# Merging two score stretches of an attention head, with other chains held back around them

## The chip, the core and the metric

The kernel runs on one core of a Trainium2 chip. The core's engines run side by side, each in its own order: PE (TensorE, matrix products; its weight loads are listed as PEld), DVE (VectorE), ACT (ScalarE), POOL (GpSimd), and SP, which issues DMAs. PE writes its products into PSUM, which has eight banks; DVE and ACT read them from there. The metric is the time of one execution in microseconds of device time, the median of several runs. A profiled execution gives, for every instruction, its start and length.

## The reference

One decoder layer, on 512 tokens of width 1024, in float32:

```
x = x + 0.5 * swiglu(rms_norm(x), ...)                  # first FFN
x = x + hybrid_mixer(rms_norm(x), ...)                  # state space part beside attention
x = x + memory_cross_attention(rms_norm(x), ...)
x = x + 0.5 * swiglu(rms_norm(x), ...)                  # second FFN
return rms_norm(x, norm_final_w)
```

The change concerns the mixer. Its attention has 8 heads; each head has two sets of queries and keys (c = 0, 1) of width 64 and a value of width 128:

```
logits = einsum('bqhcd,bkhcd->bhcqk', q_blk, k) * scale + bias   # causal, by blocks of 128 queries
p = softmax(logits)
w = p[:, :, 0] - lam * p[:, :, 1]
out = einsum('bhqk,bkhe->bqhe', w, v)
```

The other half of the mixer is a state space scan with 16 heads in 4 groups, by chunks of 128 tokens, with a gated norm over each group at its end.

## The kernel before

All products in float32 are made from operands split into a high and a low part (names that end in h and l), three products in place of one: high by high, high by low, low by high. ACT makes the high part and DVE the low one. Weights come in tiles of 128 x 1024 (wr), are split into wh and wl, and feed 24 products of 512 columns each; three wh and wl buffers stand in a row.

PSUM is cut into four banks "acc" for the large projections and four banks "aux" for everything small: scores, transposes, states, norms.

**The order of the work** comes from the class Order. It holds a list of dense generators (the projections, which yield about every second product) and a list of chains (the small work that depends on them). A chain yields how long it wants to rest; each entry of the list is a due time and the generator. The clock od.t advances with each product by a modelled cost, (columns + 8) / 2400 us for split operands, four times that for plain float32 products, and 2 x (128 + 8) / 2400 us for a transpose. The loop in run() first takes ready[0], the first chain of the list that is due, in order of spawning, and otherwise the next dense step. What is written first has the higher priority when the instructions are laid out; PE, DVE and ACT can still be given another order where an operand isn't there in time by the planner's reckoning. SP and POOL keep the written order.

**A head** is a chain (head, line 766), spawned 3.4 us after its queries and keys are projected. Its steps, with the rest between them: scores of block 3 (512 keys); 3.3; scores of block 2 (384 keys) and combine(3); 3.3; scores of blocks 1 and 0 (256 and 128 keys), combine(2) and turn(3); 3.3; combine(1), combine(0) and turn(2); 3.3; turn(1); 2.0; turn(0); 3.3; the product with the values (po); 2.08; a transpose (ptk) for the norm; 6.75; a transpose back (pot). scores (line 770) takes two aux banks, one for each c, and makes for each block three products for each c. The operands of c = 0 lie in partitions 0 to 63, those of c = 1 in 64 to 127: these are products over 64 rows, and two of them run side by side. Behind them DVE adds the bias and takes the extreme of each row (line 787), and ACT makes the exponentials and their sums (line 788). combine joins the two softmaxes on DVE, turn transposes the weights into an aux bank (pt) and splits them out of it.

A projection of queries and keys takes PE some 11 us, so the end of one head's chain lies beside the beginning of the next.

**A group** of the scan is a chain too (group, line 928). For each of its two halves j it makes decay factors on ACT and DVE (names gate and th, line 993), rests 6.9 us (2.0 more for j = 0, 0.5 more for j = 1 of group 2), and makes the products pf and py. Later sums_by_token (nps) gives the squares of each token, inv_rms_cols takes a power on POOL (ncol, line 368), and row_of (line 371) rests and then spreads the result by four transposes (nrow). DVE scales y by it (line 1028), and the parts of ys are split. The last output projection (out_proj) reads ys: of its first two tiles the first six k steps run ahead, and the last two wait for group 3.

Other chains in the same list: conv (three steps on DVE for each tile of the scan's inputs, which read an acc bank), steps (the time steps of the scan), and block_sums_in_dram, which makes sums of weight tiles in DRAM for the second FFN with a DMA on SP and an adding DMA on POOL for each.

Of the kernel before, what the change touches and what calls it, by code (L numbers as in the profile page):

```python
# [14 lines left out]
ALU = mybir.AluOpType  # L15
AX = mybir.AxisListType

P = 128
T = 512
# [18 lines left out]
W = {"h0": 3.4, "hs": 3.3, "ht": 2.0, "hv": 2.08, "hp": 6.75}  # L38
# [18 lines left out]
class Order:  # L57
# [5 lines left out]

    def __init__(self):
        self.t = 0.0
        self.dense = []
        self.chains = []

# [12 lines left out]
    def run(self):  # L81
        blocked = None
        while self.dense or self.chains:
            ready = [c for c in self.chains if c[0] <= self.t]
            if ready:
                self.step(ready[0])
                continue
            if blocked is not None and blocked():
                blocked = None
            if self.dense and blocked is None:  # L90
                try:
                    blocked = next(self.dense[0])
                except StopIteration:
                    self.dense.pop(0)
                continue
            c = min(self.chains, key=lambda c: c[0])
            self.t = max(self.t, c[0])
            self.step(c)


def body(tc, a, dbg=None):
# [31 lines left out]
    def aux(s, shape=(P, T)):  # L133
        return aux_p.tile(list(shape), F32, tag="aux", name=nm(s))
# [6 lines left out]
    V, S, G = nc.vector, nc.scalar, nc.gpsimd  # L141
    od = Order()

    def mm(out, w, x, start, stop, share=1.0):
        od.t += share * (1 if w.dtype == R32 else 4) * (x.free_size() + 8) / 2400
        newest_mm[:] = [nc.tensor.matmul(out, w, x, start=start, stop=stop).ins]  # L146
# [189 lines left out]
    for k in range(KT):  # L336
# [3 lines left out]
        w = s2("wa")  # L340
# [425 lines left out]
    def head(hd, q, kq, bias):  # L766
        es, w0, w1 = {}, {}, {}
        sm = [small("sm", 4) for _ in range(2)]

        def scores(*blocks):  # L770
            ps = [aux("ps") for _ in range(2)]
            parts, to = {}, 0
            for i in blocks:
                n = P * (i + 1)
                parts[i] = slice(to, to + n)
                to += n
                for j, (u, w) in enumerate(((0, 0), (0, 1), (1, 0))):
                    for c in range(2):
                        pc = slice(64 * c, 64 * c + 64)
                        mm(ps[c][:, parts[i]], q[u][pc, i * P : (i + 1) * P], kq[w][pc, :n], j == 0, j == 2)  # L780
            for i in blocks:
                n = P * (i + 1)
                es[i] = []
                for c in range(2):
                    ec = s2("ec", shape=(P, n))
                    mn = small("mn", 1, bufs=8)
                    V.tensor_tensor_reduce(out=ec[:, :n], in0=ps[c][:, parts[i]], in1=bias[:, T - n :], scale=0.125, scalar=3e38, op0=ALU.add, op1=ALU.min, accum_out=mn)  # L787
# [23 lines left out]
                w0[j], w1[j] = s2("wt", R32, (P, n)), s2("wt", R32, (P, n))  # L811
            split_into(w0[j], w1[j], pt[:, :n])

        scores(3)
        yield W["hs"]
        scores(2)
        combine(3)
        yield W["hs"]
        scores(1, 0)
        combine(2)  # L820
        turn(3)
        yield W["hs"]
# [12 lines left out]
        hs = slice((hd % 4) * P, (hd % 4 + 1) * P)  # L835
# [92 lines left out]
    def group(g, bt, ct, xs, zs):  # L928
# [52 lines left out]
        for j in range(2):  # L981
# [3 lines left out]
            for hh in range(2):  # L985
# [5 lines left out]
                    S.activation(r[:, c], r[:, c], AF.Relu, bias=cum[:, c, hd : hd + 1], scale=-1.0)  # L991
                S.activation(r, r, AF.Exp, scale=-1.0)
                V.tensor_tensor(r, r, cbm, ALU.mult)
            yield W["gd"] + (W["gt"] if j == 0 else 0.5 if g == 2 else 0.0)
            pf = aux("pf")
            with behind(list(newest_mm)):
                for c in range(1, 4):
# [24 lines left out]
        yield W["gq"] + (1.2 if g == 2 else 0.0)  # L1022
        pn = yield from sums_by_token(sq[0], 4)
        rh = inv_rms_cols(pn, 4, 4.0 / (4 * 256), 4.0 * EPS)
        pr = yield from row_of(rh, 4, W["gn"] + 1.1)
        for j in range(2):
            n = 2 * g + j
            V.scalar_tensor_tensor(yz[j], yz[j], par[:, C_SSD + n : C_SSD + n + 1], pr, ALU.mult, ALU.mult)
# [643 lines left out]
```

## Time and profile before

| | |
|---|---|
| median of 3 runs | 1290.15 us (1289.37 to 1290.36) |
| the profiled execution | 1289.51 us |
| its span, first to last instruction | 1287.7 us |
| granted PE clock, mean | 0.997 |
| 378 to 490 us (heads 0 to 3): PE, DVE, ACT busy | 111.97, 76.88, 62.17 us of 112 |
| 560 to 650 us (heads 4 to 7): PE, DVE, ACT busy | 90.00, 67.87, 53.56 us of 90 |
| 760 to 800 us (end of the groups): PE, DVE, ACT busy | 39.41, 31.90, 25.08 us of 40 |

A line of the timeline gives the start in us from the span's start, the length in us, the engine, the line of the kernel, the operation, what it writes and reads, the shapes (for PE the rows x columns of the array that it uses, and the moving operand), and how many like instructions the line joins. Idle time ahead of it stands in brackets with what ended it. A line of groups ends with the busy time, the mean length in ns, and the idle time ahead. Products overlap: the next one starts before the last has ended, so the length of a joined line is more than the distance to the next line.

### The profile page before, as it was taken

Reading aid. Unit: us, or ns where it says so; the run is one execution under the profiler, and the core shown is the slowest. Engines: PE = TensorE matmul, PEld = TensorE weight load, DVE = VectorE, ACT = ScalarE, POOL = GpSimd, SP = SyncE. Lnnn points to the kernel's source line nnn. Section 1 sums busy time; section 2 is a strip of 40 time slices with the busy share of each in tenths; the row PEclk is TensorE's granted clock in tenths of the full one; section 3 lists DMA queues with packets and bytes.
Section 4 is the critical chain, followed back from the end, with each engine's and each line's share of the span. In section 5 each row is a group of like instructions: output and inputs, shape, how many; then the busy total and the mean of one; then the engine's idle time right before and its main releaser. Section 6 shows DMA issues by size and latency. Waiting matters only on the chain.

```text
span 1287.7 us, 20009 instructions
## 1 busy us (share of the span) xinstructions
PE 1275.9 (99%) x7673; PEld 1115.9 (87%) x7673; DVE 969.3 (75%) x1547; ACT 708.2 (55%) x1207; POOL 111.6 (9%) x135
## 2 busy tenths in 40 slices
PE   9999999999999999999999999999999999999996
PEld 7889998998988788877888878888899899989995
DVE  6988898788875786657768697546668878877886
ACT  7545564566654564446654566434475546545554
POOL 1001010002201011101102011020001000000000
PEclk9999999999999999999999999999999999999998
DMA  9468677789865436753376457593259776666662
GB/s 338 104 173 209 180 204 203 217 217 238 284 205 159 128 74 191 214 173 84 96 224 199 137 150 241 197 229 99 69 160 243 207 222 177 193 190 187 186 202 87
DMA packets 69695, 234.70 MB, mean 182 GB/s; under 512 B 8144, under 2 KB 9568, under 8 KB 69248
## 3 DMA queue, kind: packets, MB, share of 16 engines
q1 hardware_dynamic: 53504, 181.12, 41.9%
q0 software_dynamic: 13456, 45.67, 19.8%
q10 hardware_dynamic: 2640, 6.65, 1.6%
q8 instruction: 60, 0.98, 0.3%
q14 instruction: 35, 0.29, 0.1%
HBM read 231.25 MB, written 48.29 MB: 217 GB/s over the span
## 4 chain that ended last, share of the span: by engine, by line
PE 88%; issue 9%; ACT 1%; POOL 1%; DMA 1%; DVE 1%; POOLq 0%; DVEq 0%; ACTq 0%
PE qb L244 13%; PE pm L146 9%; PE qe L244 9%; PE qa L244 8%; PE ob L1328 7%; PE oa L1328 5%; PE oe L1328 4%; PE pk L146 3%; PE pv L146 3%; PE pq L146 3%; PE pcq L146 3%; PE pxbc L146 3%; PE pck L146 2%; PE pa L146 2%; PE pg L146 2%
## 5 line engine op out<-in xcount | busy, mean ns | idle before, releaser
L155 ACT ACTIVATE wh<-wr 128x1024 fp32r<-128x1024 f32 (+1 forms) x245 | 251.2, 1028 | 223.4 <-PE qe L244 31.0
L156 DVE TENSOR_TENSOR wl<-wr,wh 128x1024 fp32r<-128x1024 f32 (+1 forms) x245 | 290.0, 1186 | 74.6 <-ACT wh L155 60.2
L1308 ACT ACTIVATE wh<-wr 128x1024 fp32r<-128x1024 f32 (+1 forms) x74 | 72.8, 984 | 65.9 <-PE ob L1328 17.4
L1317 DVE TENSOR_TENSOR wl<-wr,wh 128x1024 fp32r<-128x1024 f32 (+1 forms) x74 | 82.7, 1126 | 12.9 <-ACT wh L1308 11.0
L788 ACT ACTIVATE ec<-ec,mn 128x512 f32<-128x512 f32 (+3 forms) x64 | 35.3, 554 | 21.9 <-DVE mn L787 21.9
L787 DVE CUSTOM_DVE_ANT_0 ec<-ps,bias 128x512 f32<-128x512 f32 (+3 forms) x64 | 28.1, 487 | 16.2 <-PE ps L146 16.1
L368 POOL TENSOR_TENSOR ncol<-nv,mhalf 128x4 f32<-128x4 f32 (+1 forms) x9 | 11.4, 1271 | 299.8 <-DVE nv L366 299.8
L901 DVE SCALAR_TENSOR_TENSOR conv<-pxbc,par,conv 128x511 f32<-128x511 f32 (+2 forms) x48 | 35.8, 745 | 1.9 <-ACT conv L897 1.3
L253 POOL DMA_DIRECT2D wr<-in_f2q x11 | 9.7, 879 | 306.1 <-DMA wr<-in_f2q 230.4
L146 PE MATMUL pxbc<-hnl,wh 128*128 128x512 f32 x128 | 35.6, 405 | 0.0
L146 PE MATMUL pxbc<-hnh,wh 128*128 128x512 f32 x128 | 34.7, 398 | 0.0
L146 PE MATMUL pxbc<-hnh,wl 128*128 128x512 f32 x128 | 32.5, 393 | 0.0
L456 DVE TENSOR_TENSOR gate<-qb,row 128x512 f32<-128x512 f32 x19 | 13.1, 692 | 20.3 <-PE qb L244 20.3
L146 PEld LDWEIGHTS pxbc<-hnh,wl 128*128 128x128 f32 x128 | 23.7, 188 | 5.2 <-issue 0.2
L146 PEld LDWEIGHTS pxbc<-hnl,wh 128*128 128x128 f32 x128 | 23.1, 188 | 4.9 <-issue 0.6
L146 PEld LDWEIGHTS pxbc<-hnh,wh 128*128 128x128 f32 x128 | 23.4, 189 | 4.6 <-issue 0.3
L253 POOL DMA_DIRECT2D wr<-in_f1q x16 | 14.0, 872 | 152.3 <-DVE wl L156 44.6
L457 ACT ACTIVATE gate<-gate 128x1024 f32<-128x1024 f32 x19 | 20.1, 1057 | 10.9 <-DVE gate L456 10.9
L146 PE MATMUL pv<-wh,hnh 128*128 128x512 f32 x64 | 25.4, 398 | 0.0
L146 PE MATMUL pv<-wh,hnl 128*128 128x512 f32 x64 | 25.1, 393 | 0.0
L155 ACT ACTIVATE s24h<-s 128x512 fp32r<-128x512 f32 x30 | 18.8, 627 | 9.0 <-DVE s L214 9.0
L155 ACT ACTIVATE s31h<-s 128x512 fp32r<-128x512 f32 x30 | 18.7, 624 | 7.3 <-DVE s L212 4.2
(472 smaller groups left out, 3506.3 us busy)
## 6 DMA issues: line engine op xcount, KB each, us to landing
wr<-in_f2q SPq DMA_DIRECT2D x44, 512.0 KB, 4.3
wr<-in_f1q SPq DMA_DIRECT2D x40, 512.0 KB, 4.7
wr<-in_f1b SPq DMA_DIRECT2D x23, 512.0 KB, 6.3
isum<-in_f2q SPq DMA_DIRECT2D x22, 512.0 KB, 6.2
wr<-isum SPq DMA_DIRECT2D x22, 512.0 KB, 3.5
wsum<-in_f2b SPq DMA_DIRECT2D x20, 512.0 KB, 5.6
wr<-wsum SPq DMA_DIRECT2D x20, 512.0 KB, 4.4
wr<-in_f1q POOLq DMA_DIRECT2D x16, 512.0 KB, 6.8
```

The costliest lines, as they stand in the source:

```text
L146: newest_mm[:] = [nc.tensor.matmul(out, w, x, start=start, stop=stop).ins]
L155: S.activation(hi, src, AF.Copy),
L156: V.tensor_tensor(lo, src, hi.bitcast(F32), ALU.subtract),
L244: newest_mm[:] = [nc.tensor.matmul(out, w_[:, wc], xs[kp][which][x_], start=first and j == 0 and f == 0 and kp == 0, stop=j == 2 and kp == ...
L253: last_sum[:] = [G.dma_start(raw, m, accum_op=ALU.add).ins]
L457: S.activation(gate, gate, AF.Silu)
L787: V.tensor_tensor_reduce(out=ec[:, :n], in0=ps[c][:, parts[i]], in1=bias[:, T - n :], scale=0.125, scalar=3e38, op0=ALU.add, op1=ALU.min, ...
L788: S.activation(ec[:, :n], ec[:, :n], AF.Exp, bias=mn, scale=-1.0, accum_out=sm[c][:, i : i + 1])
L901: V.scalar_tensor_tensor(y[:, d:], ps[:, : T - d], par[:, cw + j : cw + j + 1], y[:, d:], ALU.mult, ALU.add)
L1308: recent[:] = [S.activation(hi[:, i * n : (i + 1) * n], r, AF.Copy).ins for i, r in enumerate(raw)]
L1317: recent.append(V.tensor_tensor(lo[:, ns], r, hi[:, ns].bitcast(F32), ALU.subtract).ins)
L1328: newest_mm[:] = [nc.tensor.matmul(ps, a_[:, ts], b_[:, ws], start=first and k == 0 and j == 0, stop=k == n - 1 and j == 2, skip_group_che ...
```

## The change

A head's second and third score stretches become one: scores now takes several tuples of blocks, each with a pair of aux banks of its own, writes the products of all of them, and only then the reads. The call is scores((2, 0), (1,)): blocks 2 and 0 share one pair of banks, block 1 has the other. It stands where scores(2) stood; combine(3) follows it, and combine(2) and turn(3) come one rest later, as before.

Order gets a time "quiet", before which no chain is taken. The head sets it 1.8 us behind its first scores, to od.t + 1.5, and rests for 1.5 itself; and again behind the merged stretch, to od.t + 2.0.

In a group, the second half's products of group 3 rest 0.5 us longer, as group 2's do already, and the rest ahead of nrow goes from 2.6 us to 4.1 for groups 0 to 2 and to 2.9 for group 3.

```diff
     def __init__(self):
         self.t = 0.0
+        self.quiet = 0.0
         self.dense = []
         self.chains = []
...
-            ready = [c for c in self.chains if c[0] <= self.t]
+            ready = [c for c in self.chains if c[0] <= self.t >= self.quiet]
...
             c = min(self.chains, key=lambda c: c[0])
-            self.t = max(self.t, c[0])
+            self.t = max(self.t, c[0], self.quiet)
             self.step(c)
...
-        def scores(*blocks):
-            ps = [aux("ps") for _ in range(2)]
-            parts, to = {}, 0
-            for i in blocks:
-                n = P * (i + 1)
-                parts[i] = slice(to, to + n)
-                to += n
-                for j, (u, w) in enumerate(((0, 0), (0, 1), (1, 0))):
-                    for c in range(2):
-                        pc = slice(64 * c, 64 * c + 64)
-                        mm(ps[c][:, parts[i]], q[u][pc, i * P : (i + 1) * P], kq[w][pc, :n], j == 0, j == 2)
-            for i in blocks:
+        def scores(*pairs):
+            parts = {}
+            for blocks in pairs:
+                ps, to = [aux("ps") for _ in range(2)], 0
+                for i in blocks:
+                    n = P * (i + 1)
+                    parts[i] = [p_[:, to : to + n] for p_ in ps]
+                    to += n
+                    for j, (u, w) in enumerate(((0, 0), (0, 1), (1, 0))):
+                        for c in range(2):
+                            pc = slice(64 * c, 64 * c + 64)
+                            mm(parts[i][c], q[u][pc, i * P : (i + 1) * P], kq[w][pc, :n], j == 0, j == 2)
+            for i in parts:
...
-        scores(3)
+        scores((3,))
+        yield W["hs"] - 1.5
+        od.quiet = od.t + 1.5
+        yield 1.5
+        scores((2, 0), (1,))
+        combine(3)
+        od.quiet = od.t + 2.0
         yield W["hs"]
-        scores(2)
-        combine(3)
-        yield W["hs"]
-        scores(1, 0)
         combine(2)
         turn(3)
         yield W["hs"]
...
-            yield W["gd"] + (W["gt"] if j == 0 else 0.5 if g == 2 else 0.0)
+            yield W["gd"] + (W["gt"] if j == 0 else 0.5 if g > 1 else 0.0)
...
-        pr = yield from row_of(rh, 4, W["gn"] + 1.1)
+        pr = yield from row_of(rh, 4, W["gn"] + (2.6 if g < 3 else 1.4))
```

More of the change, by code (lines that the diff above doesn't have):

```diff
@@ L786, in scores @@
                     mn = small("mn", 1, bufs=8)
-                    V.tensor_tensor_reduce(out=ec[:, :n], in0=ps[c][:, parts[i]], in1=bias[:, T - n :], scale=0.125, scalar=3e38, op0=ALU.add, op1=ALU.min, accum_out=mn)
+                    V.tensor_tensor_reduce(out=ec[:, :n], in0=parts[i][c], in1=bias[:, T - n :], scale=0.125, scalar=3e38, op0=ALU.add, op1=ALU.min, accum_out=mn)
                     S.activation(ec[:, :n], ec[:, :n], AF.Exp, bias=mn, scale=-1.0, accum_out=sm[c][:, i : i + 1])
```

## The prediction

> **What bounds the kernel now.** First the page's busy times, then the waits of PE.
>
> ```profile
> span 1287.7 us, 20009 instructions
> PE 1275.9 (99%) x7673; PEld 1115.9 (87%) x7673; DVE 969.3 (75%) x1547; ACT 708.2 (55%) x1207; POOL 111.6 (9%) x135
> ```
>
> ```profile
> PE nrow L150 <- POOL ncol L368: 0.5, 1, 0.5
> ```
>
> PE is the bound; beside one wait at the start, the view of waits knows a single one on PE, 0.5 us at a nrow. What else PE loses must lie inside its "busy" time, whose ends are modelled. So I read distances between starts in PE's timeline. A long run of projections gives the pitch, (801.29 - 799.47) / 8 = 0.2275 us for 512 columns:
>
> ```profile
> 799.47 1.98 PE L146 MATMUL pm<-ysh,wh 128*128 128x512 f32 x8
> 801.29 1.98 PE L146 MATMUL pm<-ysl,wh 128*128 128x512 f32 x8
> ```
>
> Now head 1's second and third score stretches, pairs of 64-row products among full ones:
>
> ```profile
> 427.09 0.61 PE L146 MATMUL pk<-hnh,wh 128*128 128x512 f32 x2
> 427.63 0.44 PE L146 MATMUL ps<-kh,qh 64*128 64x384 f32 x2
> 427.91 0.34 PE L146 MATMUL ps<-kl,qh 64*128 64x384 f32 x2
> 428.08 0.34 PE L146 MATMUL ps<-kh,ql 64*128 64x384 f32 x2
> 428.35 1.65 PE L146 MATMUL pk<-hnh,wh 128*128 128x512 f32 x6
> 429.84 1.52 PE L146 MATMUL pk<-hnl,wh 128*128 128x512 f32 x6
> 431.29 0.38 PE L146 MATMUL ps<-kh,qh 64*128 64x256 f32 x2
> ...
> 431.81 0.28 PE L146 MATMUL ps<-kl,qh 64*128 64x128 f32 x2
> 431.92 0.28 PE L146 MATMUL ps<-kh,ql 64*128 64x128 f32 x2
> 432.13 0.33 PE L150 MATMUL pt<-ident,ec 128*128 128x128 f32 x1
> 432.21 0.71 PE L146 MATMUL pk<-hnl,wh 128*128 128x512 f32 x2
> 432.76 0.62 PE L146 MATMUL pk<-hnh,wl 128*128 128x512 f32 x2
> ```
>
> A pair of 384 columns in the middle takes 428.08 - 427.91 = 0.17. Entering: the two pk last 0.54 instead of 0.455 (+0.09), the first pair 0.28 (+0.11). Leaving: the last pair 0.27 (+0.10), the six pk 1.49 instead of 1.365, of which about 0.02 is their usual loss (+0.10). **A stretch costs 0.40 us beyond its columns**, while PE counts as busy. There are three a head, eight heads.
>
> **The change, part by part.** *Merging.* One stretch a head goes: -0.40. Nothing else fills that time, since PE is the bound on both sides. The merged stretch does the same columns: its 128-column pairs were already paced at 0.11 (431.81 to 431.92), and stay so.
>
> Against it: turn(3)'s one transpose stood right behind the old third stretch. There leaving (0.21 - 0.11 = 0.10), the transpose (0.08) and the slow start of the two pk behind (0.55 - 0.455 = 0.10) make 0.28. Afterwards it stands alone: leaving into projections costs 0.20, and a lone transpose looks like this:
>
> ```profile
> 790.73 0.27 PE L150 MATMUL nps<-ident,nsum 128*128 128x128 f32 x1
> 790.75 1.62 PE L146 MATMUL pm<-ysh,wl 128*128 128x512 f32 x6
> 792.21 1.52 PE L146 MATMUL pm<-ysh,wh 128*128 128x512 f32 x6
> ```
>
> 0.02 for itself and 1.46 - 1.365 = 0.10 behind, so 0.32 altogether, 0.04 more. **Net 0.36 a head, 2.9 us for eight clean heads.**
>
> The Trainium skill ("TensorE: Matmul & The Clock Gate", Single matmul latency) puts the latency of a lone warm matmul at (398 + N)/2.4 ns, 166 ns besides its columns. If each change of tiling exposed that much, an estimate would be 0.33 for entering and leaving, 2.7 us before the transposes' share. The rows show 0.40, so the sum goes by the rows.
>
> *The four banks.* The merged stretch needs all four aux banks at once, where each old one needed two. The head's own first pair is no danger:
>
> ```profile
> 456.29 0.50 PE L146 MATMUL ps<-kh,qh 64*128 64x512 f32 x2
> ```
>
> ```profile
> 458.39 0.69 DVE L787 CUSTOM_DVE_ANT_0 ec<-ps,bias 128x512 f32<-128x512 f32 x1
> ```
>
> Head 3's first scores start at 456.29, their second read ends at 459.08, 2.8 us on; the merged stretch starts about 3.4 after the first one and wants these banks one part later. Others are danger. The hold lifts at od.t + 1.5, and the head's own step is due at the same od.t + 1.5. Order.run then takes ready[0], the chain spawned first: **a step of the previous head that was held goes immediately ahead of the stretch.** Where is one held? Head 2's hold is set 1.3 (modelled cost of six 512-column scores) + 1.8 = 3.1 after its first scores start. Head 1's turn(1) follows those scores at once; its three transposes cost 0.34, turn(0) is due 2.0 later, at 1.3 + 0.34 + 2.0 = 3.64: held, then first. Head 5 stands to head 4 the same way. In the trace turn(0) is already there:
>
> ```profile
> 441.69 0.60 PE L150 MATMUL pt<-ident,ec 128*128 128x128 f32 x4
> 442.22 0.44 PE L146 MATMUL ps<-kh,qh 64*128 64x384 f32 x2
> ```
>
> ```profile
> 443.04 0.68 DVE L156 TENSOR_TENSOR wt<-pt,wt 128x512 fp32r<-128x512 f32 x1
> ```
>
> Its bank comes free at 443.72. Behind 442.22, the 384-column pairs (0.28 + 0.17 + 0.17) and the 128-column ones (0.06 + 0.11 + 0.11) last until 443.12, when the last pair of banks is wanted. So PE waits 0.6, with all projections queued behind it, or projections are put in between, which costs another 0.40. Bounds for such a head: -0.36 (free in time) to +0.25 (waits); I take 0, near the second case. Heads 0, 1 and 4 have no head before them in work. In heads 3 and 6 the previous turn(0) comes before the hold, 1.5 us and more ahead. **Six times 0.36 = 2.2 us.**
>
> *What is held back.* A hold lasts up to 1.5 + 2.0 (the stretch's modelled cost) + 2.0 = 5.5. Held steps of heads 3 and 7 have no later head to hold them, so the output projections wait for nothing new. The sums in DRAM (their SP and POOL DMAs too) slip by at most 8 x 5.5 = 44 us:
>
> ```profile
> L1280 POOL DMA_DIRECT2D isum<-isum x11: 812/862/1755, 414.6 to 853.7; - x11
> ```
>
> ```profile
> L251 SPq DMA_DIRECT2D wr<-isum x22: 319/326/333, 915.9 to 1205.4; - x22
> ```
>
> The last isum is issued at 853.7, the first is read at 915.9: 62 us. Cost 0; were that cover gone, the second FFN would wait for the difference. On DVE six reads come in one go, 8 x 0.487 - 2 x 0.69 = 2.5 us:
>
> ```profile
> L787 DVE CUSTOM_DVE_ANT_0 ec<-ps,bias 128x512 f32<-128x512 f32 (+3 forms) x64 | 28.1, 487 | 16.2 <-PE ps L146 16.1
> ```
>
> Weight splits behind them feed a tile of 24 x 0.2275 = 5.5 us of PE, three buffers deep: hidden, else up to 2.5. A conv chain that is held keeps its acc bank for 3 x 0.9 + 5.5 = 8.2 instead of 2.7; the other three banks last PE 16.4 us: hidden too. The ec tiles of blocks 1 and 0 live one stage longer, four of the sixteen half-size slots, with at most two heads in work: 0. Reading blocks 0 and 1 a stage earlier takes nothing off the path, because no head's chain is on it. combine(3) stands behind six reads on DVE instead of two, four more of 0.487 or less, up to 1.9 us; turn(3), which needs it, is due 3.3 after the stretch: 0.
>
> *The nrow of group 2.*
>
> ```profile
> 759.40 1.17 PE L146 MATMUL pcv<-wh,hm 128*128 128x512 f32 x4
> 761.02 0.65 PE L150 MATMUL nrow<-ident,ncol 128*128 128x128 f32 x4 [0.45 <-POOL ncol L368]
> ```
>
> ```profile
> 759.93 1.03 POOL L368 TENSOR_TENSOR ncol<-nv,mhalf 128x4 f32<-128x4 f32 x1 [52.54 <-DVE nv L366]
> ```
>
> Four pcv with their slow start take 1.01, so nrow was up at 760.41 and waited 0.6 for POOL. Put 1.5 later (4.1 for 2.6) it comes up at 761.9, ncol being there since 760.96, with pcv work to fill. **-0.6**; bounds 0 (another wait takes its place) and -0.6. Behind nrow DVE scales y and splits it into ys; for groups 0 to 2 these are read first by the last output projection (the pm<-ysh rows near 790 above), some 25 us on: 0. The nrows of groups 0 and 1 showed no wait, and lose none.
>
> *Group 3.* Its second py comes 0.5 later, its nrow 0.3.
>
> ```profile
> 780.52 1.07 PE L146 MATMUL pcv<-wh,hm 128*128 128x512 f32 x4
> 781.73 1.09 PE L146 MATMUL py<-th,xdt 128*64 128x128 f32 x16
> ```
>
> ```profile
> 780.99 0.69 DVE L993 TENSOR_TENSOR th<-th,cbm 128x512 f32<-128x512 f32 x1
> ...
> 795.65 1.35 DVE L156 TENSOR_TENSOR ysl<-y,ysh 128x512 fp32r<-128x512 f32 x2
> ```
>
> ```profile
> 797.21 0.61 PE L146 MATMUL pm<-ysl,wh 128*128 128x512 f32 x2
> ```
>
> py waited until th was done (781.68): 1.21 less 0.91 and 0.09 of switching, 0.2. That goes. But the last ysl ends at 797.00 and its product is up at 797.21 + 0.23 = 797.44: 0.44 of slack, against 0.8 later less the 0.2. Up to 0.2 is late next. I take 0 for both together, bounds -0.2 and +0.4.
>
> **Sum:** -2.2 - 0.6 = -2.8 us. The profiled execution took 1289.51 (its span 1287.7 and 1.8 around it), so 1286.7; it lies 0.64 under the median shown, 1290.15, from which the same 2.8 leads to **1287.4 us**, -0.22%.
>
> **The rivals.**
>
> *All eight heads clean* and py's 0.2 kept: 2.9 + 0.6 + 0.2 = 3.7, 1286.5. For it: 443.72 is only 0.6 after the bank is wanted, and a held turn(0) could come out earlier. Against it: the list order above.
>
> *The stretch isn't one stretch.* Banks are free too late by the planned order, projections land between the two pairs, and the entering and leaving that were to go are back. Then only the nrow is left: -0.6, 1289.5. For it: PE's order already differs from the due times in places, and heads 3 and 6 have transposes of others shortly ahead (pot, turn(0)). Against it: those banks are read within about 2 us.
>
> *PE waits for banks* (slower). Place: what comes first behind a stretch and needs an aux bank: po, pot or another's turn at the end of the hold. In head 7 the reads fell far behind:
>
> ```profile
> 620.38 0.39 PE L146 MATMUL ps<-kh,qh 64*128 64x256 f32 x2
> ```
>
> ```profile
> 624.45 0.28 DVE L787 CUSTOM_DVE_ANT_0 ec<-ps,bias 128x128 f32<-128x128 f32 x1
> ```
>
> From the first product to the last read 4.3 us; with two 384-column reads more about 5.3. The hold ends 1.5 + 2.0 = 3.5 after the start, so a bank can be 1.8 late, and PE runs in order. At three heads this eats the gain and 2.6 more: it decides from there; at all five with chains behind (2, 3, 5, 6, 7) it is 9.0 - 2.8 = +6.2, 1296.4. Against it: in this trace PE never waits for a bank. The Trainium skill ("TensorEngine Tiling (Array Packing)", PSUM Bottleneck) says just this, that packing speeds up TensorE and not the emptying of PSUM; the trace bears it out only as DVE's lag, not yet as a wait of PE.
>
> **How the numbers follow.** Forecast 0.42, all clean 0.18, split stretch 0.27, waits for banks 0.13. 0.2% is 2.6 us, about what a measurement can tell from no change: below 1287.6. The forecast's own range, 1286.6 to 1288.2, straddles it, six parts in ten below: 0.25 + 0.18 = 0.43 faster; 0.17 + 0.27 = 0.44 the same; 0.13 slower. Range: 1286.0 (all clean, with 0.5 of scatter) to 1290.3 (split, and 0.4 lost in group 3 and more scatter); the waits for banks are left out.
>
> **What would show it.** Right: two entries to 64-row products a head, not three, 0.40 each; in heads 2 and 5 turn(0) right ahead and projections or a gap inside the stretch; no POOL wait at nrow. Wrong: pm waiting for ysl near 797; PE waits named ps, po or pot released by DVE; projections between the 128- and 256-column pairs in other heads too.

## The result and the profile after

The kernel after takes **1294.86 us** (median of 6 runs, 1293.56 to 1295.70) and the kernel before, on the same chip, 1290.37 (6 runs, 1289.37 to 1290.91): a ratio of 1.0037, 95% interval 1.0025 to 1.0048. It is slower by 4.5 us, where 2.8 us of gain were forecast; the time lies outside the stated range. The profiled execution took 1295.41.

The page of after, span and busy times:

```profile
span 1293.6 us, 20016 instructions
...
PE 1277.6 (99%) x7673; PEld 1118.7 (86%) x7673; DVE 968.3 (75%) x1547; ACT 707.9 (55%) x1207; POOL 113.8 (9%) x135
```

No engine has more instructions to run. The view of PE's waits (us in total, times, the longest), where before had one line besides a wait at the start, which both have:

```profile
PE ps L147 <- DVE wt L157: 1.4, 4, 0.4
PE ps L147 <- DVE rl L800: 0.9, 2, 0.5
PE qb L245 <- DVE c L312: 0.8, 1, 0.8
PE nrow L151 <- POOL ncol L369: 0.8, 1, 0.8
PE pt L151 <- DVE wt L157: 0.4, 1, 0.4
```

Six waits of scores (ps) are new, one of a transpose (pt), one in the second FFN (qb); the wait of nrow has not gone but grown.

Where the time went is read from stretches between two instructions with the same work between them. For heads 2 and 3 these are head 2's first scores and the first pcb of the scan. PE's timeline of before, then of after:

```profile
438.55 0.50 PE L146 MATMUL ps<-kh,qh 64*128 64x512 f32 x2
...
493.85 1.05 PE L146 MATMUL pcb<-th,th 128*128 128x128 f32 x8
```

```profile
439.35 0.50 PE L147 MATMUL ps<-kh,qh 64*128 64x512 f32 x2
...
496.48 1.05 PE L147 MATMUL pcb<-th,th 128*128 128x128 f32 x8
```

55.30 us have become 57.13: heads 2 and 3 lose 1.83. The table reads the other heads in the same way, from like instruction to like instruction, for the kernels that change the heads (us against before). The columns' work is the same in every row, and profiles of equal head code agree closely (after, after_again and sums_free within 0.1 in each part), so these differences can be read to some 0.1, where the total time scatters by 1 or 2:

| kernel | head 0 | head 1 | heads 2, 3 | head 4 | heads 5 to 7 | all |
|---|---|---|---|---|---|---|
| before, length | 49.32 | 14.31 | 55.30 | 28.92 | 73.26 | |
| after | +0.10 | -0.28 | +1.83 | -0.31 | +1.98 | +3.32 |
| after_again | +0.10 | -0.28 | +1.77 | -0.31 | +2.07 | +3.35 |
| sums_free | +0.06 | -0.23 | +1.80 | -0.31 | +2.03 | +3.35 |
| three_heads | +0.13 | -0.28 | 0.00 | -0.31 | -0.05 | -0.51 |
| crowded_heads | 0.00 | 0.00 | +1.71 | 0.00 | +3.09 | +4.80 |
| own_first | +0.10 | -0.28 | +0.04 | -0.31 | -0.34 | -0.79 |
| no_hold | +0.39 | -0.16 | +2.52 | -0.17 | +1.98 | +4.56 |
| early_turn | -0.17 | -0.23 | +1.66 | -0.31 | +2.63 | +3.58 |
| turn_at_once | +0.03 | -0.28 | +6.38 | -0.31 | +7.18 | +13.04 |
| ptk_apart | 0.00 | +0.03 | +0.07 | 0.00 | +0.06 | +0.16 |
| acc_pair | +0.09 | -0.23 | +0.13 | -0.31 | +0.42 | +0.10 |
| acc_best_hold | +0.10 | -0.28 | +0.18 | -0.31 | +0.44 | +0.13 |
| acc_nohold | +0.38 | -0.28 | +2.62 | -0.31 | +1.81 | +4.22 |
| own_first_best | +0.12 | -0.23 | -0.07 | -0.31 | -0.53 | -1.02 |
| merged_best | +0.11 | -0.28 | -0.09 | -0.31 | -0.50 | -1.07 |
| best_acc20 | +0.09 | -0.23 | -0.48 | -0.31 | -0.53 | -1.46 |
| best_acc | +0.09 | -0.28 | -0.33 | -0.31 | -0.53 | -1.36 |

In after, heads 1 and 4 bring 0.28 and 0.31 each, near the forecast 0.36; heads 2, 3 and 5 to 7 cost 3.8. Besides the heads, after's profiled span is longer by 0.22 at the groups' end, 1.07 in the second FFN, 0.98 in the first 27 us (where these kernels scatter by 1.2 with the same instructions), and 0.3 elsewhere: 5.9 in all, 1293.6 - 1287.7.

Head 2's merged stretch in PE's timeline of after, with the turn(0) of head 1 ahead of it:

```profile
442.95 0.60 PE L151 MATMUL pt<-ident,ec 128*128 128x128 f32 x4
443.48 0.44 PE L147 MATMUL ps<-kh,qh 64*128 64x384 f32 x2
...
444.40 0.33 PE L147 MATMUL ps<-kh,qh 64*128 64x256 f32 x1
445.17 0.38 PE L147 MATMUL ps<-kh,qh 64*128 64x256 f32 x1 [0.44 <-DVE wt L157]
...
445.71 0.96 PE L147 MATMUL pk<-hnh,wh 128*128 128x512 f32 x3
```

Of the pair at 444.40 only one product runs; the other, which needs the last bank, starts 0.77 later. DVE at that time:

```profile
442.69 1.23 DVE L157 TENSOR_TENSOR wl<-wr,wh 128x1024 fp32r<-128x1024 f32 x1 [0.56 <-PE pq L147]
443.83 0.68 DVE L161 SCALAR_TENSOR_TENSOR ql<-pq,qh 128x512 fp32r<-128x512 f32 x1
444.43 0.68 DVE L157 TENSOR_TENSOR wt<-pt,wt 128x512 fp32r<-128x512 f32 x1
```

turn(0)'s bank comes free when DVE has split it, at 445.11, and a weight split and the split of q stand ahead. Head 3 is worse, since turn(1) was still in its bank too. (The view names rl for that wait, as the latest thing on DVE; DVE's split of turn(1), a wt of 384 columns, ended at 462.96, just ahead of 463.11. Which bank a tile gets is inferred from the order in which the kernel asks for aux tiles.)

```profile
461.57 0.44 PE L147 MATMUL ps<-kh,qh 64*128 64x384 f32 x2
...
463.11 0.35 PE L147 MATMUL ps<-kh,qh 64*128 64x256 f32 x1 [0.46 <-DVE rl L800]
463.75 0.38 PE L147 MATMUL ps<-kh,qh 64*128 64x256 f32 x1 [0.28 <-DVE wt L157]
...
464.29 0.98 PE L147 MATMUL pxbc<-hnh,wh 128*128 128x512 f32 x3
```

From its first pair to the projection behind, the stretch lasts 445.71 - 443.48 = 2.23 in head 2 and 464.29 - 461.57 = 2.72 in head 3. The same stretch without a wait lasts 1.41 (own_first and acc_pair, below). So the waits cost 0.8 and 1.3; heads 5 and 6 repeat both. Together that is 4.2, more than the 3.8 that heads 2, 3 and 5 to 7 lose.

### The profile page after: what moved, and what is told of

It is laid out like the page before. It is cut to its first block, busy times and chain, and to the rows that moved or that the text cites. A ratio compares the mean times of both kernels' runs of the same rounds, so it can differ in the third digit from the quotient of the medians.

```text
span 1293.6 us, 20016 instructions
## 1 busy us (share of the span) xinstructions
PE 1277.6 (99%) x7673; PEld 1118.7 (86%) x7673; DVE 968.3 (75%) x1547; ACT 707.9 (55%) x1207; POOL 113.8 (9%) x135
## 4 chain that ended last, share of the span: by engine, by line
PE 87%; issue 9%; DVE 2%; POOL 1%; ACT 1%; DMA 0%; POOLq 0%; DVEq 0%; ACTq 0%
PE qb L245 13%; PE pm L147 9%; PE qe L245 8%; PE qa L245 8%; PE ob L1332 7%; PE oa L1332 5%; PE oe L1332 4%; PE pcq L147 3%; PE pk L147 3%; PE pq L147 3%; PE pxbc L147 3%; PE pv L147 3%; PE pck L147 2%; PE pa L147 2%; PE pcv L147 2%
## 5 line engine op out<-in xcount | busy, mean ns | idle before, releaser
L860 POOL TENSOR_TENSOR rr<-ev,mhalf 128x4 f32<-128x4 f32 x8 | 11.0, 1372 | 170.8 <-DVE ev L858 170.8
```

## The experiments

The theory: a merged stretch wants all four aux banks within 0.9 us, finds one or two of them taken by the previous head's turns, and PE waits, with every projection queued behind. The rivals: the loss comes from the group edits, from the holds, from the DMAs that are held, or from the merging itself.

**Which heads, and which part.** Three kernels that do one part alone.

```diff
# three_heads: before, with the change's lines in Order and scores, and in head
+        if hd in (0, 1, 4):
...
+            od.quiet = od.t + 1.5
+            yield 1.5
+            scores((2, 0), (1,))
...
+        else:
...
+            scores((1, 0))
# crowded_heads: the same with
+        if hd in (2, 3, 5, 6):
# groups_only: before, and
-            yield W["gd"] + (W["gt"] if j == 0 else 0.5 if g == 2 else 0.0)
+            yield W["gd"] + (W["gt"] if j == 0 else 0.5 if g > 1 else 0.0)
-        pr = yield from row_of(rh, 4, W["gn"] + 1.1)
+        pr = yield from row_of(rh, 4, W["gn"] + (2.6 if g < 3 else 1.4))
```

> Merged stretch and holds only in heads 0, 1 and 4, which have no other head's chain in work; groups as before. Theory (a bank filled by a held step of the previous head is what costs): the merged stretches of these heads show about 0.57 us beyond their columns and no wait, each head saves about 0.36 us net, together -1.1 us, about 1289.3. Rival 1 (six reads in one go on DVE and ACT cost, whatever else holds a bank): waits or late transposes here too, 0 or slower. Rival 2 (the heads are innocent, held DMAs of the sums or the start cost the 4.5 us): no clear change either, but no wait inside a stretch.

> Merged stretch and holds only in heads 2, 3, 5 and 6; groups as before. Theory: turn(0) of the head before stands right ahead of each of the four stretches and its bank isn't free when the last pair is wanted: waits of about 0.6 us (heads 2, 5) and 1.1 us (heads 3, 6) as in the changed kernel, against 4 x 0.36 saved, and some single transposes that stand alone: +2 to +3 us, 1292.4 to 1293.4. Rival 2: about -1 to 0.

> The kernel before with the two later steps of the groups alone. By the forecast nrow of group 2 no longer waits for POOL: -0.6 us, about 1289.8. By what the changed kernel's trace shows (nrow waits 0.78 us there, more than before): the wait stays, 0 to +0.4 us.

three_heads took 1290.0 us, a ratio of 0.9998 (0.9990 to 1.0007); crowded_heads 1295.67, 1.0041 (1.0028 to 1.0055); groups_only 1290.48, 1.0001 (0.9992 to 1.0010). The loss is in the four heads that have another head's turns beside them: crowded_heads alone is at least as slow as after, with the same waits in its stretches. It loses more than the 2 to 3 us expected. Part of that stands behind head 7's first scores (1.1 longer than in after), where head 7's old stretches remain and a pot waits 0.5. three_heads gains less than the expected 1.1: in the table, heads 1 and 4 bring 0.28 and 0.31 each, but head 0 brings nothing. The group edits bring nothing either; nrow waits 0.8 in groups_only as in after, and from the first pcb of group 2 to the ys products they make groups_only 0.29 longer.

**The order alone.** When the hold lifts, the head that set it steps first, and the others after it.

```diff
# own_first: after, and in Order's step (c is the chain that has just stepped)
+            if c is self.owner:
+                self.owner = None
...
+            if self.claim:
+                self.claim, self.owner = False, c
# Order's run
-            ready = [c for c in self.chains if c[0] <= self.t >= self.quiet]
+            ready = [c for c in self.chains if c[0] <= self.t >= self.quiet and self.owner in (None, c)]
# head
-        od.quiet = od.t + 1.5
+        od.quiet, od.claim = od.t + 1.5, True
```

> The changed kernel, but when a hold ends the head that set it takes its step before any chain that was held. Theory: heads 2 and 5 then show a stretch like heads 0, 1 and 4 (0.57 us beyond the columns instead of 1.28); in heads 3 and 6 a ptk now stands some 4.7 us ahead, whose bank was held 5.9 to 7.3 us in the kernel before, so a wait of 0.3 to 1.7 us stays there, on ptk's release and not on wt. Together 1.4 us less than the changed kernel from heads 2 and 5, and up to 2 us less from 3 and 6: 1291.5 to 1293.5. Rival 1: waits inside the stretches of heads 2 and 5 stay.

1289.89 us, 0.9994 (0.9985 to 1.0003). The view of PE's waits has one line besides the start:

```profile
PE nrow L156 <- POOL ncol L374: 0.8, 1, 0.8
```

No stretch waits, all eight last about 1.42 us, and heads 2, 3 and 5 to 7 come out 4.1 us shorter than in after. That is better than expected, since the wait on ptk in heads 3 and 6 did not come. But the eight heads gain only 0.79 of the 2.9 that eight clean heads were to bring.

**Without the holds.** The merging stays.

```diff
# no_hold: after, and
-        od.quiet = od.t + 1.5
-        od.quiet = od.t + 2.0
```

> Edit: the kernel after without its two hold lines; the merged stretch stays. Theory (the loss is made by the hold and the list order together: the hold collects the previous head's turn(0), which then takes a bank right ahead of the stretch): the planner still puts turn(0) of the previous head right ahead of the merged stretch in heads 2, 3, 5 and 6, so waits for banks stay, 1292 to 1296 us. Rival (the hold alone makes them): without it the heads come out at own_first's 1289.9 or better.

1294.59 us, 1.0034 (1.0021 to 1.0046): as slow as after, but not in the same places. In heads 2 and 5 turn(0) stands right ahead of the stretch without the holds too, and the stretches last 2.09 and 2.10 us. In heads 3 and 6, against the expectation, turn(0) comes 2.9 us ahead, and the stretches run through in 1.41. Head 3 on PE:

```profile
458.88 0.66 PE L151 MATMUL pt<-ident,ec 128*128 128x128 f32 x4
...
461.75 0.44 PE L147 MATMUL ps<-kh,qh 64*128 64x384 f32 x2
```

Instead, po now stands behind a stretch and waits:

```profile
PE po L147 <- ACT ec L790: 2.9, 3, 1.1
```

```profile
464.82 0.28 DVE L789 CUSTOM_DVE_ANT_0 ec<-ps,bias 128x128 f32<-128x128 f32 x1
```

```profile
465.26 0.82 PE L147 MATMUL po<-wt,vh 128*128 128x512 f32 x4 [1.13 <-ACT ec L790]
```

The view names an Exp, but po reads nothing that these exponentials write. By the order of the aux tiles, po takes the first bank of the stretch, and the last read of that bank by DVE (the row shown) ends 0.16 us ahead of po, the same in all three waits. So this too looks like a wait for a bank, though the view doesn't say so.

So the holds make the bank waits of heads 3 and 6 (2.6 of the 4.2 us), but not those of heads 2 and 5. Without them the loss moves to po: in these runs the merged stretch costs where another step that needs an aux bank stands close beside it.

**Moving turn(0) away on PE.** Two kernels change the rest between turn(1) and turn(0).

```diff
# early_turn: after, and
-        yield W["ht"]
+        yield W["ht"] - 1.4
         turn(0)
# turn_at_once: after, and
-        yield W["ht"]
         turn(0)
```

> Edit: the kernel after with the rest before turn(0) 1.4 shorter. In heads 2 and 5 the previous head's turn(0) then comes eight projections ahead of the merged stretch, in heads 3 and 6 still right ahead of it. Theory (a stretch waits because a bank taken right ahead of it isn't free when its last pair of banks is wanted): in heads 2 and 5 the stretch costs 0.57 to 0.6 beyond its columns instead of 1.28, without a wait; in heads 3 and 6 it stays at 1.8; the time is some 1.4 below after. Rival (the waits come from the stretch's own first scores or from DVE being behind in general): all four stretches keep their waits.

> Edit: the kernel after without the rest between turn(1) and turn(0). In heads 2 and 5 the seven transposes then come right behind the next head's first scores, and eight projections ahead of its merged stretch; what follows in heads 3 and 6 is rearranged. Theory (the bank comes free where DVE reads it: behind the two reads of the first scores and ahead of DVE's wait for Exp, if the transposes are up by then): the stretches of heads 2 and 5 cost 0.6 and have no wait. Rival (only the distance on PE counts, and eight projections were too few in early_turn): they wait 0.6 as there.

Both expectations failed. early_turn (1293.67 in its one run) put eight projections between turn(0) and the stretches of heads 2 and 5, and these still waited: they last 2.15 and 2.17 us. Its time is 1.2 below after, near the expected 1.4, but by luck: its heads are 0.26 longer than after's, and against after's profile it gains 0.94 in the first 27 us, which scatter, and 1.1 in the second FFN. turn_at_once (1303.94) put seven transposes at once behind the first scores, and head 2's wait grew. Its PE:

```profile
440.20 0.98 PE L151 MATMUL pt<-ident,ec 128*128 128x128 f32 x7
...
443.85 0.33 PE L147 MATMUL ps<-kh,qh 64*128 64x256 f32 x1
445.03 0.36 PE L147 MATMUL ps<-kh,qh 64*128 64x256 f32 x1 [0.84 <-DVE wt L157]
```

The transposes are done by 441.2, 2.7 us ahead of the pair that waits for their bank. ACT and DVE, through which the bank has to come free (ACT makes the high part, DVE the low one):

```profile
441.88 0.71 ACT L790 ACTIVATE ec<-ec,mn 128x512 f32<-128x512 f32 x1
...
442.59 0.58 ACT L156 ACTIVATE wt<-pt 128x512 fp32r<-128x512 f32 x1
```

```profile
443.05 1.23 DVE L157 TENSOR_TENSOR wl<-wr,wh 128x1024 fp32r<-128x1024 f32 x1
444.20 0.68 DVE L157 TENSOR_TENSOR wt<-pt,wt 128x512 fp32r<-128x512 f32 x1
```

ACT first makes the next head's two exponentials (the row shows the second), so its copy ends at 443.17; then DVE's split stands behind a weight split, and the bank is free at 444.88. In these two runs, how far the transposes stand ahead on PE counts for little: the bank's release hangs on what stands ahead of its two readers on ACT and DVE. In heads 3 and 6 the stretch ran into ptk's bank instead, and waited 2.5.

**The bank alone.** Nothing is moved; the last pair of banks comes from the accumulators' pool. (Head 0 is left out: there the values' projection holds all four acc banks.)

```diff
# acc_pair: after, and in scores
-                ps, to = [aux("ps") for _ in range(2)], 0
+                ps, to = [(acc if blocks == (1,) and hd else aux)("ps") for _ in range(2)], 0
```

> Edit: the kernel after, with the two banks of block 1's scores taken from the accumulators' pool (heads 1 to 7; head 0 as in after). PE's order is that of after. Theory (the stretches wait for an aux bank that a held step still occupies, and for nothing else): the waits of 0.6 and 0.5 in heads 2, 3, 5 and 6 are gone, each of these stretches costs 0.5 to 0.6 beyond its columns, heads 2 and 3 come out 1.9 shorter than in after and heads 5 to 7 2.0 to 2.5 shorter; about 1291.0 us. Rival (something else of the merged stretch makes PE wait): 1294.5 with the same waits.

1290.71 us, 1.0004 (0.9995 to 1.0013), 4.15 below after. PE's waits, besides the start:

```profile
PE nrow L151 <- POOL ncol L369: 0.8, 1, 0.8
PE ptk L151 <- ACT of L847: 0.7, 4, 0.2
PE pt L151 <- DVE wt L157: 0.4, 1, 0.4
```

With turn(0) right ahead as in after, every stretch runs through in about 1.42. This settles the loss: it is the bank. Heads 2 and 3 come out 1.70 shorter than in after and heads 5 to 7 1.56, less than the expected 1.9 and 2.0 to 2.5. The run also shows what the merging gives back once no bank is short, four waits of ptk for "of", the copy of po:

```profile
448.72 0.57 ACT L847 ACTIVATE of<-po 128x512 f32<-128x512 f32 x1
```

```profile
449.35 0.66 PE L151 MATMUL ptk<-ident,of 128*128 128x128 f32 x4 [0.15 <-ACT of L847]
```

po was done by 448.4, but ACT had six exponentials in one go (from 445.75 to 448.72), and "of" is the next in its order. In before, the third stretch stood between po and ptk:

```profile
447.46 0.60 ACT L843 ACTIVATE of<-po 128x512 f32<-128x512 f32 x1 [1.92 <-PE po L146]
```

```profile
447.35 0.39 PE L146 MATMUL ps<-kh,qh 64*128 64x256 f32 x2
...
448.35 0.60 PE L150 MATMUL ptk<-ident,of 128*128 128x128 f32 x4
```

There PE worked on scores while ACT copied. The stretch that was merged away was cover. In heads 2 and 3 of acc_pair the products ahead of ptk lose 0.69 us beyond their pitch, in heads 5 to 7 0.78; head 7's pt waits 0.4. Without these waits the two and the three heads would gain 0.56 and 0.76, some 0.27 a head.

**Standing alone.** Is it the waiting, or only that ptk stands alone among projections? Before, with the rest ahead of ptk 1.4 longer in heads 1, 2, 5 and 6, whose ptk stand in the work of heads 2, 3, 6 and 7:

```diff
# ptk_apart: before, and
-        yield W["hv"]
+        yield W["hv"] + (1.4 if hd % 4 in (1, 2) else 0.0)
```

> Edit: before with one rest longer (1.4 more ahead of the output row's transposes in the middle heads), so that ptk no longer stands right behind the third stretch and its lone transpose but alone among projections, in heads 2, 3, 5 and 6. Nothing else is added. Theory (what stood beside the old third stretch shared its break in the projections, and pays for a break of its own once it stands alone): +0.1 to +0.2 a head, so heads 2 and 3 together and heads 5 to 7 each +0.2 to +0.4 longer. Rival (standing alone costs 0.04 as the prediction had it for the lone transpose): both within 0.1 of before.

One run of 1290.24; heads 2 and 3 are 0.07 longer, 5 to 7 0.06. The rival is right: standing alone costs about 0.03, as the prediction had it.

**nrow.** Before, with a much longer rest for group 2 alone:

```diff
# nrow_far: before, and
-        pr = yield from row_of(rh, 4, W["gn"] + 1.1)
+        pr = yield from row_of(rh, 4, W["gn"] + 1.1 + (8.0 if g == 2 else 0.0))
```

> Edit: before with one change, the rest before group 2's nrow 8.0 longer instead of 1.5 (nrow then has 13 other matmuls ahead of it behind the second nps). Theory (the 1.5 did not reach past POOL's ncol): the 0.5 to 0.8 wait on POOL is gone, -0.5 us, 1289.9. Rival (the wait costs nothing or another takes its place): 1290.4 and no segment between groups 2 and 3 shorter.

1289.97 us, 0.9996 (0.9987 to 1.0005); the groups' end is 0.58 shorter, the same size as the forecast 0.6, though the total can't tell it from no change. PE in after, with the rest 1.5 longer, then in nrow_far:

```profile
763.72 0.27 PE L151 MATMUL nps<-ident,nsum 128*128 128x128 f32 x1
763.75 0.95 PE L147 MATMUL pm<-yah,wl 128*128 128x512 f32 x3
765.47 0.65 PE L151 MATMUL nrow<-ident,ncol 128*128 128x128 f32 x4 [0.78 <-POOL ncol L369]
```

```profile
760.65 0.27 PE L150 MATMUL nps<-ident,nsum 128*128 128x128 f32 x1
...
765.35 0.60 PE L150 MATMUL nrow<-ident,ncol 128*128 128x128 f32 x4
```

In after nrow still stands three products behind nps, although its rest alone is 4.1 us: it seems that the squares were summed late, so that the rest had run out before, and that the order of PE went by what was reckoned to be ready, without POOL's 1.14 us. This reading is argued from the order, not tested apart.

**The held DMAs.** After, with the chain that sums blocks in DRAM free of the holds:

```diff
# sums_free: after, and in Order and where the chain is spawned
+    def spawn(self, gen, after=0.0, free=False):
+            ready = [c for c in self.chains if c[0] <= self.t and (c[2] or self.t >= self.quiet)]
+        od.spawn(block_sums_in_dram(), 10.0, True)
```

> Edit: the kernel after, with the chain that sums blocks in DRAM free of the holds. PE's order is that of after. Theory A (the second FFN's late weight tile, +1.07 us there in after, comes from DMAs that the holds delay): about 1293.8, -1.0 against after, with no PE wait on c near 994. Rival B (that wait is a chance of the DMA queues, or comes from heads that are late): 1294.9 with it or without it. In both the eight heads stay 3.3 longer than before.

> Edit: none, the kernel after once more, for the second FFN. Theory A (the weight tile that came 1.07 us late there is late by the order of the DMAs on POOL's queue): the wait on c near 994 comes again, 0.7 to 1.1 us. Rival B (a chance of one execution): it is gone or under 0.3. The heads come out as in after in both.

after_again is the kernel after, unchanged. sums_free: 1294.32 us, 1.0028 (1.0017 to 1.0038), no wait on c, 1.07 less in the second FFN, heads as in after. after_again: 1294.59 in one run, also without that wait. In after, POOL's queue and what came late:

```profile
967.23 0.87 POOL L1284 DMA_DIRECT2D wsum<-in_f2b  x1
975.13 0.90 POOL L254 DMA_DIRECT2D wr<-in_f2q  x1 [7.03 <-DVE wl L157]
```

```profile
984.15 1.06 ACT L156 ACTIVATE wh<-wr 128x1024 fp32r<-128x1024 f32 x1 [3.43 <-DMA wr<-in_f2q]
```

In after and seven more of the nine kernels with held sums, a wsum transfer stands ahead of this weight tile on POOL; in three_heads, which has holds in three heads alone, and in before and sums_free it stands behind. Over all profiled executions, this part of the second FFN is longer than in before by 1.07, 0.52, 0.52, 0.36 and 0.16 us in five of the eight with that order, and by less than 0.03 in the other three, in three_heads and in the ten further kernels whose sums were free. So the held sums make a wait possible that comes in some executions, about 0.3 us on the mean; that the order on POOL is the reason is argued, not shown. With the same order, after issues this load 8.9 us behind the last ncol on POOL (975.13) and after_again 6.15 us (972.65); so something besides this order delayed it in after.

**Towards a better version.** The first two take up own_first, the others acc_pair; in all four the group edits are undone and group 2's nrow rests 8.0 longer.

```diff
# own_first_best: own_first, and
-        yield W["hv"]
+        yield W["hv"] + (0.6 if hd % 4 in (1, 2) else 0.0)
-            yield W["gd"] + (W["gt"] if j == 0 else 0.5 if g > 1 else 0.0)
+            yield W["gd"] + (W["gt"] if j == 0 else 0.5 if g == 2 else 0.0)
-        pr = yield from row_of(rh, 4, W["gn"] + (2.6 if g < 3 else 1.4))
+        pr = yield from row_of(rh, 4, W["gn"] + 1.1 + (8.0 if g == 2 else 0.0))
# merged_best: own_first_best, and as in sums_free
+        od.spawn(block_sums_in_dram(), 10.0, True)
# acc_best_hold: acc_pair with both lines of group and the sums as here
# acc_nohold: acc_best_hold, and
-        od.quiet = od.t + 1.5
-        od.quiet = od.t + 2.0
```

> Edit: own_first (the head that set the hold steps first when it lifts), both group edits undone, the output row that follows po put 0.6 later in the middle heads, and the rest before group 2's nrow 8.0 longer. Theory (merged stretch worth 0.35 a head where all four banks are free; about 2 us of that is given back by short groups that stood behind the old third stretch and now stand alone, ptk waiting 0.2 for its operand among them; nrow's place on PE is fixed by what the planner reckons as ready, so that only a long rest moves it past POOL): about 1289.0 us, -1.2 to -1.6 against before, no PE wait named nrow, ptk not late. Rival (the loss is not in ptk and not in nrow): 1289.8 to 1290.0, as own_first.

> Edit: own_first_best with the chain that sums blocks in DRAM free of the holds. Theory A (the sums held back move a DMA on POOL's queue ahead of a weight tile): the 0.5 us wait on c in the second FFN is gone; about 1288.4 us, ratio 0.9984. Rival B: 1289.1 as own_first_best, ratio 0.9989.

> Edit: acc_pair, both group edits undone, the rest before group 2's nrow 8.0 longer, and the sums in DRAM free of the holds. Theory: as acc_pair and the nrow's 0.6 and the group edits' 0.2 to 0.3 less: 1290.0 to 1290.3 if the heads come out as in before, 1288.0 if the merged stretch brings 0.3 a head now that its neighbours can stand beside it.

> Edit: acc_best_hold without the two hold lines. Theory (the holds were there to keep other chains off the banks; with banks to spare they are not needed, and other chains can stand right beside a stretch): no wait for a bank, heads no longer than in acc_best_hold; 1288 to 1289 us. Rival (without a hold others take banks in the stretch as in no_hold, where po waited 1.3 for Exp): 1290 or more.

own_first_best took 1289.15 us, 0.9989 (0.9980 to 0.9998), merged_best **1288.27, 0.9986 (0.9977 to 0.9995)**, a small gain over before. Against own_first, the heads of own_first_best are 0.23 shorter and its groups' end 0.92, so little came back of the 2 us that the expectation put down to short groups standing alone. The one wait of PE beyond 0.3 that is left is that at the start. acc_best_hold took 1289.98, 0.9999 (0.9990 to 1.0008): its stretches are as short, but ptk waits for "of" as in acc_pair. acc_nohold took 1294.14, 1.0029 (1.0018 to 1.0041), where 1288 to 1289 were expected; po and the stretches no longer wait, but this came:

```profile
PE ptk L151 <- ACT of L845: 5.1, 4, 1.4
```

So the holds do have a use: they keep po off the stretch's banks (no_hold), and ptk from standing where ACT has six exponentials ahead of the copy that it needs (acc_nohold).

In merged_best one stretch, head 3's, lasts longer than the others, though the view of waits shows nothing. PE in merged_best, from the first pair to the projection behind:

```profile
457.73 0.63 PE L152 MATMUL ps<-kh,qh 64*128 64x384 f32 x2
...
459.54 0.96 PE L152 MATMUL pxbc<-hnh,wl 128*128 128x512 f32 x3
```

1.81 us instead of 1.42; the two products of the first pair last 0.63 together instead of 0.44, since one starts 0.19 late. Two kernels give one pair of the stretch banks of the other pool.

```diff
# best_acc20: merged_best, and
-                ps, to = [aux("ps") for _ in range(2)], 0
+                ps, to = [(acc if blocks == (2, 0) and hd else aux)("ps") for _ in range(2)], 0
# best_acc: the same with (1,) in place of (2, 0)
```

> Edit: merged_best with the banks of blocks 2 and 0 (the stretch's first pair) taken from the accumulators' pool in heads 1 to 7. Theory (in head 3 the first pair gets one bank of the head's own first scores 0.2 late, its two products fall out of step, and the stretch runs 0.4 longer): the pairs of head 3 are in step, heads 2 and 3 are 0.4 shorter than in merged_best; about 1287.9 us, ratio 0.9982. Rival (the pairs fall out of step for another reason): head 3 as in merged_best, 1288.3.

> Edit: the same with the banks of block 1 (the stretch's last pair) instead. Theory: the first pair still takes the late bank, so head 3 stays out of step and heads 2 and 3 are as in merged_best; 1288.3 us. Rival: in step as well.

The same two rows in best_acc20, then in best_acc:

```profile
457.42 0.44 PE L152 MATMUL ps<-kh,qh 64*128 64x384 f32 x2
...
458.83 0.96 PE L152 MATMUL pxbc<-hnh,wl 128*128 128x512 f32 x3
```

```profile
458.25 0.63 PE L152 MATMUL ps<-kh,qh 64*128 64x384 f32 x2
...
459.85 0.73 PE L152 MATMUL pxbc<-hnh,wl 128*128 128x512 f32 x2
```

1.41 and 1.60. best_acc20 is in step, and heads 2 and 3 are 0.39 shorter than in merged_best, as expected. best_acc stays out of step, but gains 0.24, which neither theory had: so the 0.4 of merged_best are two late banks, the first pair's (1.60 - 1.41, pairs out of step) and the last pair's (1.81 - 1.60). In merged_best the second product of the 256-column pair starts at 459.00, 0.06 behind DVE's split of the previous head's turn(1), which ended at 458.94. The total times, 1288.55 (0.9988, 0.9979 to 0.9997) and 1288.33 (0.9988, 0.9979 to 0.9997), can't be told from merged_best's.

## Why the prediction was wrong

The profiled execution took 8.7 us more than the 1286.7 forecast for it: 5.5 in the heads, 0.8 at the end of the groups (0.22 lost for a forecast gain of 0.6), 1.1 in the second FFN, 1.0 in the first 27 us, which scatter, and 0.3 elsewhere.

**Merging, "Net 0.36 a head": near in size in heads 1 and 4.** They brought 0.28 and 0.31. In head 0, which is alone too, 0.36 was forecast and 0.1 was lost; the products just ahead of pcum lose 0.1 more there and those around po 0.25, which was seen in PE's distances and not tested.

**"A step of the previous head that was held goes immediately ahead of the stretch": right, and the failed step stands behind it.** "In heads 3 and 6 the previous turn(0) comes before the hold, 1.5 us and more ahead" is wrong. It was read from the order of before; in after, turn(0) stands right ahead in heads 3 and 6 too, with turn(1) still in its bank. Without the holds turn(0) does come 2.9 us ahead (no_hold). With them turn(1) comes only behind head 3's first scores (at 458.86, where before had it ahead of them at 454.96), so turn(0), due 2.0 later, falls into the hold as in head 2; why turn(1) slid was not traced. These two heads were taken at -0.36 each, and their stretches alone wait 1.3. In heads 2 and 5 the forecast weighed -0.36 against +0.25 and took 0, "near the second case"; the waits of 0.8 make it worse than the second case. It was named that the bank would come free 0.6 after it is wanted; that came near (the second product starts 0.77 late), and the 0 was chosen against one's own row. The waits in these four heads are 4.2 of the 5.5 us between forecast and result in the heads (-2.2 against +3.3).

**The place of the rival.** "PE waits for banks" had a chance of 0.13 and 1296.4 us; that this is close to what came is luck, since it looked behind the stretch, at po, pot or a turn of another chain. There a bank wait came once in after (pt in head 7, 0.4). Inside the stretch it came in four heads. The place that the rival named does show without the holds: po's waits in no_hold. The Trainium skill ("TensorEngine Tiling (Array Packing)", Gotcha 1: PSUM Pressure) says that tiles of rows write to different banks and so press on PSUM; acc_pair shows it here with a price, 4.15 us between the same stretch with and without two more banks. The Trainium skill ("PSUM — Partial Sum Buffer", PSUM bank collisions raise a hardware error) gives the reason, that tiles of rows may not write one bank at the same time; no run here shows that.

**"What is held back ... 0": half right.** No wait of PE in after or acc_pair is put down to DVE's six reads, and on DVE combine(3) even came ahead of them. But the forecast counted what the merging does to DVE and not to ACT: six exponentials in one go delay "of", and ptk with it, 1.5 us in heads 2, 3 and 5 to 7 of acc_pair. No wait shows the sums' cover of 62 us used up, yet their transfers are issued in another order in the second FFN.

**"Put 1.5 later ... it comes up at 761.9": wrong, with the size right.** The wait is worth 0.6 (nrow_far: 0.58); a rest of 1.5 doesn't reach it, 8.0 does. **Group 3, "0 for both together, bounds -0.2 and +0.4":** the edits in the groups, all together, make the groups' end 0.2 to 0.3 longer in after and groups_only, within these bounds. The wait of py on th did go: the view has 0.2 for it in three_heads and crowded_heads, which lack the group edits, and nothing in after.

## What to carry to other kernels

Before two short uses of a small pool are merged, list who holds each buffer at the moment the merged use wants the last one, in the order that the change itself makes, and price the release by what stands ahead of the buffer's readers on their engines, not by how early it was written. Where a row says that a buffer comes 0.6 too late, the sum takes 0.6, and every product queued behind pays it. A short stretch between two dependent steps may be the cover for the copy that joins them: taking it away moves its cost to the next wait.

## What was not expected of the hardware

Two 64-row products that start together run side by side: a pair of 384 columns takes 0.17 us, which is what the pitch of 0.2275 us for 512 columns gives for one product. A bank that is 0.2 us late for one of them sets the pairs out of step, and they stay so through the pairs behind, which costs 0.19 us for the same products (best_acc against best_acc20). The view of waits shows nothing of it, since PE is busy throughout.
